# A chain of four transformer parts on one core: another routing tail, one-hot spread and norm, and first products on both halves of the tokens at once

## The chip, the cores and the metric

The kernel runs on one core of one Trainium2 chip. A core has TensorE (PE in the rows; PEld is its loading of weights), VectorE (DVE), ScalarE (ACT), GpSimd (POOL) and SyncE (SP), which work from queues of their own, 16 DMA engines, an SBUF of 128 partitions and the PSUM into which matmuls accumulate. The metric is the device time of one execution in microseconds (us), the median of the runs.

## The reference

256 tokens of width 1024 pass through five parts, each added to its input: a convolution and gated linear attention ("even"), a PEER layer, a gated softmax attention ("odd"), a second PEER layer, and a block with sparse and stick-breaking attention and a feed-forward part (1024 to 4096 to 1024, relu squared). The change touches the two PEER layers, the norms and the feed-forward part:

```python
def peer_ffn(h, wq, keys, u, v):
    q = (h @ wq).reshape(B, S, PEER_HEADS, 2, half)
    s1 = jnp.einsum('bshd,hnd->bshn', q[..., 0, :], keys[:, 0])
    s2 = jnp.einsum('bshd,hnd->bshn', q[..., 1, :], keys[:, 1])
    v1, i1 = lax.top_k(s1, 16)
    v2, i2 = lax.top_k(s2, 16)
    cand = (v1[..., :, None] + v2[..., None, :]).reshape(B, S, 8, 256)
    sc, j = lax.top_k(cand, 16)
    e1 = jnp.take_along_axis(i1, j // 16, axis=-1)
    e2 = jnp.take_along_axis(i2, j % 16, axis=-1)
    experts, gates = e1 * 128 + e2, jax.nn.softmax(sc, axis=-1)
    ...
    act = jax.nn.gelu(jnp.einsum('td,ted->te', ht, u[et]))
    return jnp.einsum('te,ted->td', gt * act, v[et])

    # feed-forward part of the last block
    ff = jnp.square(jax.nn.relu(u2 @ mlp_w1)) @ mlp_w2
```

## The kernel before

**Products.** All large products are taken with f32 split in a high and a low part (`split`, L98 on ScalarE for the high part, L101 for the low part on VectorE or GpSimd), in three matmuls: high by high, high by low, low by high. `hH` and `hL` are the parts of the normed tokens, transposed: 128 rows of the width by 256 tokens for each of KD = 8 pieces. `wload` fetches 512 KB of weights for two products and splits them (`hu`/`lu` and `hv`/`lv` by the ring of buffers in turn); `K.rings` says which engine takes a ring's low parts.

**A PEER layer** (`peer`) computes all 16384 experts densely, as 128 row blocks of 128 hidden units, and gates them by a matrix G that is zero but for the chosen experts. `first(n)` takes 24 matmuls of 256 columns (L768) into `pA` and a Gelu into `A` (L771); `gated(n)` multiplies by G and splits the product into CH and CL (L776, L98, L101); `second(n)` adds the product with v in 12 matmuls of 512 columns (L790, L791, L794) into `po`. 40 first products (RUN) of each half of 64 row blocks are taken ahead, during the routing and the spread; the other 24 stand in the loop over n, so 48 per layer and 96 in the kernel. In the loop a step is one `gated`, one `first` and one `second`, and in the second layer every other step has a piece of the next block's modulation (`ada.one`, L1062).

**Routing** (`routing`) searches the 16 best of the scores by rounds of MAX, MATCH_REPLACE and MAX_INDEX on VectorE. Behind the last search stands the tail: the places j become row and column numbers (L712 to L718), each as a mask against 16 ranks (L734) times the indices (L737), summed by 16 matmuls (L739) per 128 tokens and kind; the softmax gates (L722 to L727) are turned by TensorE (L731). `ahead(5)` puts five first products in front of these on TensorE, `ahead(3)` three more in between.

**Spread** (`spread`): in 32 steps of 8 tokens VectorE builds one-hots of the row number (L811), of the column number (L813) and the first times the gates' high and low parts (L816, twice); 16 small matmuls (L825) make G of them. Three of four steps take one of the first products.

**Norms** (`norm_rows`): per 128 tokens scale, transpose, split to hH and hL; between them the weights of the next products are split. The last block's feed-forward part takes its first products in `gemm_T`, 24 matmuls of 256 columns (L163), then relu and square.

The order on each engine is that of the program, but for the places where `issue_after` and `keep_in_program_order` set it. The lines that set the order in the tail:

```python
    for t in range(2):
        ahead(5 - 2 * t)
        tp = K.ps.tile([128, 3, 128], F, name="pB")
        nc.tensor.transpose(tp[:, 2], e[:, t], K.ident)
        for k in range(2):
            ...
```

Of the kernel before, what the change touches and what calls it, by code (L numbers as in the profile page):

```python
# [30 lines left out]
KD = 8  # L31
S = 256
# [12 lines left out]
class Kit:  # L45


    def __init__(self, ctx, tc, I):
# [23 lines left out]
        self.hH = self.cst.tile([128, KD, S], R, name="hH")  # L72
        self.hL = self.cst.tile([128, KD, S], R, name="hL")
# [21 lines left out]
    def split(self, H, L, src, eng=None):  # L95
# [5 lines left out]
        return (eng or nc.vector).tensor_sub(L, src, H.bitcast(F))  # L101
# [16 lines left out]
    def wsplit(self, raw, ring, n, parts=(0, 1), eng=None):  # L118
# [3 lines left out]
        for i in parts:  # L122
            m = min(1024, n - 1024 * i)
            if m > 0:
                H.append(pool.tile([128, 1024], R, name="h" + ring))
                L.append(pool.tile([128, 1024], R, name="l" + ring))
                with self.tc.issue_after(self.hold.pop().ins) if self.hold and not self.pinning else nullcontext():
                    self.split(H[-1][:, :m], L[-1][:, :m], raw[i][:, :m], eng or own)
# [16 lines left out]
    def gemm_T(self, w, groups, xH, xL, evac, kd=KD, ring=None, psum=None, tags=("pA",), share=1):  # L145
# [5 lines left out]
        for g0 in range(groups[0], groups[1], per):  # L151
            n = min(per, groups[1] - g0)
            H, L = self.wload(w[:, g0:g0 + n].rearrange("p a b -> p (a b)"), ring, n * kd * 128)
            for i in range(n):
# [10 lines left out]
                evac(g0 + i, out)  # L165

# [68 lines left out]
    def norm_rows(self, g, shift=None, early=(), after=None, sooner=False):  # L235
# [8 lines left out]
        W, outs = [], []  # L244
        if sooner:
            self.pinning = True
            W = [self.wsplit(*w, eng=nc.vector) for w in raw]
# [3 lines left out]
        for tb in range(2):  # L251
# [9 lines left out]
            elif after is not None:  # L261
# [3 lines left out]
                else:  # L265
                    self.next = [self.wsplit(*nxt, eng=nc.gpsimd)]
# [13 lines left out]
            if not tb and not sooner:  # L280
# [342 lines left out]
def routing(K, l, grid, rt, new_psum, e1T, e2T, gP, ahead):  # L623
# [10 lines left out]
    nc.gpsimd.tensor_copy(grid, K.iota[:, :, None].to_broadcast([128, 128, 2]))  # L634
# [58 lines left out]
    for h in range(1, 8):  # L693
# [15 lines left out]
    jj = rt.tile([128, 2, 2, 128], U32)  # L709
    jb = rt.tile([128, 2, 2, 128], B)  # L710
    Jf = J.rearrange("p t h r -> p t (h r)")
    nc.vector.tensor_scalar(jj[:, 0], Jf, 4, None, op0=OP.logical_shift_right)  # L712
    nc.vector.tensor_scalar(jj[:, 1], Jf, 2, None, op0=OP.logical_shift_right)
    nc.vector.scalar_tensor_tensor(jb[:, 0], jj[:, 1], -9.0, jj[:, 0], op0=OP.add, op1=OP.max)
    nc.vector.tensor_scalar(jj[:, 0], Jf, 3, None, op0=OP.bitwise_and)
    nc.vector.tensor_scalar(jj[:, 1], Jf, 12, None, op0=OP.bitwise_and)
    nc.vector.scalar_tensor_tensor(jj[:, 1], Jf, 48.0, jj[:, 1], op0=OP.is_lt, op1=OP.mult)
    nc.vector.tensor_add(jb[:, 1], jj[:, 0], jj[:, 1])  # L718
    e = rt.tile([128, 2, 128])
    sm = rt.tile([128, 2, 8])  # L720
    g = e.rearrange("p t (a b) -> p t a b", b=16)
    nc.vector.tensor_sub(g, SC, SC[:, :, :, 0:1].to_broadcast([128, 2, 8, 16]))  # L722
    nc.scalar.activation(g, g, AF.Exp)
    nc.vector.tensor_reduce(sm, g, axis=AX.X, op=OP.add)
    nc.vector.reciprocal(sm, sm)
    nc.vector.tensor_scalar(sm, sm, GATE, None, op0=OP.mult)
    nc.vector.tensor_mul(g, g, sm[:, :, :, None].to_broadcast([128, 2, 8, 16]))  # L727
    for t in range(2):
        ahead(5 - 2 * t)
        tp = K.ps.tile([128, 3, 128], F, name="pB")  # L730
        nc.tensor.transpose(tp[:, 2], e[:, t], K.ident)  # L731
        for k in range(2):
            eq = eqs[t][k]
            nc.vector.tensor_tensor(eq, jb[:, k, t].rearrange("p (h r) -> p h r", r=16)[:, None]  # L734
# [5 lines left out]
        ts = slice(t * 128, t * 128 + 128)  # L740
        nc.scalar.activation(e1T[:, ts], tp[:, 0], AF.Copy)
        nc.scalar.activation(e2T[:, ts], tp[:, 1], AF.Copy)
        nc.scalar.activation(gP[:, 0, ts], tp[:, 2], AF.Copy)
        nc.vector.tensor_sub(gP[:, 1, ts], tp[:, 2], gP[:, 0, ts])


def peer(K, l, ada=None):
    tc, nc, I = K.tc, K.nc, K.I
    hH, hL = K.hH, K.hL
    with tc.tile_pool(name="pe", bufs=1) as pe, tc.tile_pool(name="pw", bufs=2) as pw:  # L750
        G = pe.tile([128, HALF, S], F, name="G")
        e1T, e2T = (pe.tile([128, S], B, name=n) for n in ("e1T", "e2T"))
# [857 lines left out]
```

## Time and profile before

| what | us |
|---|---|
| median of 3 runs (lowest, highest) | 2345.95 (2345.46, 2348.6) |
| the profiled execution | 2346.62 |
| its span | 2344.8 |
| TensorE busy in the span | 2293.3 (98%) |
| VectorE busy | 1595.6 (68%) |
| ScalarE busy | 1262.6 (54%) |
| GpSimd busy | 714.3 (30%) |
| weight loads of TensorE | 2080.4 (89%) |

The mean granted clock of TensorE is 0.992 of full speed. The profile is of one execution; the span runs from its first to its last instruction. A busy TensorE is not a TensorE at its best: the time between the starts of two matmuls tells what one costs, since their recorded durations overlap. In the rows below "x24" is the count of equal instructions in a row, the time behind it is that of all of them, and a bracket tells how long the engine stood idle before and who ended that.

### The profile page before, as it was taken

What the parts mean: (1) busy time and instruction counts of PE and PEld (TensorE: products, weight loads), DVE (VectorE), ACT (ScalarE), POOL (GpSimd) and SP (SyncE); (2) the same over time, 40 slices, a digit from 0 to 9 for tenths busy, and PEclk for the clock granted to TensorE, in tenths of its full rate; (3) what the DMA queues carried; (4) which work ended last, traced back from release to release, by engine and by line L of the source; (5) the groups of instructions that cost most, each with busy time, mean ns of one, the idle gap of its engine ahead of it and who ended that gap; (6) DMA issues with size and microseconds to landing.
All of it is one profiled execution on the core that took longest, in us unless ns stands there. A gap on an engine that the chain in (4) does not pass through costs nothing.

```text
span 2344.8 us, 43309 instructions
## 1 busy us (share of the span) xinstructions
PE 2293.3 (98%) x17000; PEld 2080.4 (89%) x17000; DVE 1595.6 (68%) x3124; ACT 1262.6 (54%) x2046; POOL 714.3 (30%) x327
## 2 busy tenths in 40 slices
PE   9999899999999999999989999999999999998999
PEld 8879799988999988887979998899999888887997
DVE  6949898566875556644789955679555663667754
ACT  6654455555555555675455555555555554565542
POOL 4236203444001444552840244410044442300000
PEclk9999999999999999999989999999999999999999
DMA  6235346655456665642634676554666565334652
GB/s 244 90 131 176 127 145 243 237 200 193 163 169 234 236 214 195 212 135 66 205 127 150 207 244 211 195 177 152 223 234 223 198 206 184 131 108 152 220 195 91
DMA packets 119387, 424.63 MB, mean 181 GB/s; under 512 B 14155, under 2 KB 17037, under 8 KB 118798
## 3 DMA queue, kind: packets, MB, share of 16 engines
q1 hardware_dynamic: 119180, 421.86, 53.4%
q8 instruction: 133, 2.18, 0.4%
q14 instruction: 72, 0.59, 0.1%
q10 hardware_dynamic: 2, 0.00, 0.0%
HBM read 420.72 MB, written 2.66 MB: 181 GB/s over the span
## 4 chain that ended last, share of the span: by engine, by line
PE 45%; DVE 5%; ACT 1%; issue 0%; DMA 0%; POOL 0%; SPq 0%; ACTq 0%; POOLq 0%; DVEq 0%
PE pA L768 14%; PE pA L163 5%; PE po L791 5%; PE po L794 5%; PE po L790 5%; PE pB L163 2%; PE pB L825 1%; PE pA L204 1%; PE pA L205 1%; PE pA L203 1%; PE pB L205 1%; PE pB L204 1%; PE pB L203 1%; DVE G L653 1%; DVE G L650 1%; DVE G L651 1%
## 5 line engine op out<-in xcount | busy, mean ns | idle before, releaser
L101 POOL TENSOR_TENSOR lu<-raw,hu 128x1024 fp32r<-128x1024 f32 x229 | 569.0, 2488 | 1164.9 <-ACT hu L98 1046.3
L98 ACT ACTIVATE hu<-raw 128x1024 fp32r<-128x1024 f32 x348 | 368.3, 1060 | 347.6 <-PE pA L768 248.7
L98 ACT ACTIVATE hv<-raw 128x1024 fp32r<-128x1024 f32 x340 | 360.0, 1060 | 198.7 <-PE pA L768 87.3
L101 DVE TENSOR_TENSOR lv<-raw,hv 128x1024 fp32r<-128x1024 f32 x310 | 386.3, 1248 | 91.7 <-ACT hv L98 88.5
L768 PE MATMUL pA<-hH,hu 128*128 128x256 f32 x1408 | 398.7, 283 | 2.1 <-ACT A L771 1.7
L768 PE MATMUL pA<-hH,lu 128*128 128x256 f32 x1408 | 394.2, 280 | 0.9 <-DVE lu L101 0.6
L768 PE MATMUL pA<-hL,hu 128*128 128x256 f32 x1408 | 393.6, 280 | 0.0
L101 DVE TENSOR_TENSOR CL<-AG,CH 128x256 fp32r<-128x256 f32 x256 | 205.9, 805 | 258.0 <-PE po L794 132.0
L768 PEld LDWEIGHTS pA<-hH,hu 128*128 128x128 f32 x1408 | 264.6, 188 | 6.3 <-ACT A L771 2.1
L768 PEld LDWEIGHTS pA<-hH,lu 128*128 128x128 f32 x1408 | 267.7, 190 | 2.2 <-DVE lu L101 1.5
L768 PEld LDWEIGHTS pA<-hL,hu 128*128 128x128 f32 x1408 | 265.3, 188 | 3.4
L790 PE MATMUL po<-hv,CH 128*128 128x512 f32 x688 | 267.7, 390 | 0.0
L791 PE MATMUL po<-lv,CH 128*128 128x512 f32 x688 | 267.5, 389 | 0.0
L98 ACT ACTIVATE CH<-AG 128x256 fp32r<-128x256 f32 x256 | 106.8, 418 | 271.2 <-PE po L791 268.4
L794 PE MATMUL po<-hv,CL 128*128 128x512 f32 x688 | 211.9, 389 | 0.0
L101 DVE TENSOR_TENSOR lu<-raw,hu 128x1024 fp32r<-128x1024 f32 x119 | 145.5, 1223 | 62.5 <-ACT hu L98 61.6
L768 PE MATMUL pA<-hH,hv 128*128 128x256 f32 x640 | 183.0, 286 | 0.0
L768 PE MATMUL pA<-hH,lv 128*128 128x256 f32 x640 | 178.7, 279 | 0.0
L768 PE MATMUL pA<-hL,hv 128*128 128x256 f32 x640 | 178.5, 279 | 0.0
L794 PEld LDWEIGHTS po<-hv,CL 128*128 128x128 f32 x688 | 129.2, 188 | 26.8
L791 PEld LDWEIGHTS po<-lv,CH 128*128 128x128 f32 x688 | 129.1, 188 | 23.2
L790 PEld LDWEIGHTS po<-hv,CH 128*128 128x128 f32 x688 | 129.0, 188 | 23.1
(641 smaller groups left out, 5224.9 us busy)
## 6 DMA issues: line engine op xcount, KB each, us to landing
raw<-in_p_u_dram SPq DMA_DIRECT2D x256, 512.0 KB, 3.6
raw<-in_p_v_dram SPq DMA_DIRECT2D x256, 512.0 KB, 4.4
raw<-in_b_m_dram SPq DMA_DIRECT2D x64, 512.0 KB, 3.6
raw<-in_b_ada_dram SPq DMA_DIRECT2D x48, 512.0 KB, 3.4
raw<-in_b_wT_dram SPq DMA_DIRECT2D x33, 512.0 KB, 3.3
raw<-in_p_wq_dram SPq DMA_DIRECT2D x32, 512.0 KB, 3.9
raw<-in_od_wT_dram SPq DMA_DIRECT2D x17, 512.0 KB, 3.5
raw<-in_ev_wT_dram SPq DMA_DIRECT2D x13, 512.0 KB, 6.0
```

Of the source, the lines that this page charges most:

```text
L98: i = nc.scalar.activation(H, src, AF.Copy)
L101: return (eng or nc.vector).tensor_sub(L, src, H.bitcast(F))
L163: nc.tensor.matmul(out, a, b[:, k], start=c == 0, stop=c == 3 * kd - 1)
L203: nc.tensor.matmul(po[tb][c], x, h, start=i == 0 and k == 0, stop=False)
L204: nc.tensor.matmul(po[tb][c], x, l, start=False, stop=False)
L205: nc.tensor.matmul(po[tb][c], y, h, start=False, stop=last and k == 3)
L650: nc.vector.max_index(io[:, 0:8], vo[:, 0:8], src)
L651: nc.vector.match_replace(w, vo[:, 0:8], src, LOWEST)
L768: nc.tensor.matmul(ps, a[:, ks], b[:, k], start=c == 0, stop=c == 23)
L790: nc.tensor.matmul(po[tb][dh], CH[:, ts], H[:, ds], start=n == 0, stop=False)
L791: nc.tensor.matmul(po[tb][dh], CH[:, ts], L[:, ds], start=False, stop=False)
L794: nc.tensor.matmul(po[tb][dh], CL[:, ts], H[:, ds], start=False, stop=n == 127)
```

## The change

Five things are changed. (1) The tail of the routing takes the tokens' halves and the two kinds one after the other: numbers, mask and product for k = 0, then for k = 1, with the gates behind the masks of the first half and their transpose last; from the tail on, VectorE takes the low parts of both rings; the wider candidates are spread over the last two heads. (2) In the spread the three compares become one operation over a table `eT` of the row number and the column number, this one stored two times,, and the two products with the gates one. (3) `both` is new: a product in 16 matmuls, 8 of a high weight with hH and hL side by side (512 columns, into two halves of a PSUM tile) and 8 of a low weight with hH (256 columns); ScalarE copies one half and VectorE adds the other. The 96 first products of the loops and 28 of the feed-forward part's 32 row blocks go this way; the first products ahead stay as they were, and C has three buffers instead of four. (4) hH and hL are two halves of one tile. (5) In the norms the low parts of the next weights go from GpSimd to VectorE, behind hL, and where `sooner` is set only the first part of the weights is split early.

The diff, cut to its core:

```diff
-        self.hH = self.cst.tile([128, KD, S], R, name="hH")
-        self.hL = self.cst.tile([128, KD, S], R, name="hL")
+        self.hh = self.cst.tile([128, 2, KD, S], R, name="hh")
+        self.hH, self.hL = self.hh[:, 0], self.hh[:, 1]
...
+    def both(self, out, parts, tag):
+
+
+        nc = self.nc
+        p = self.ps.tile([128, 2, S], F, name=tag)
+        for k in range(KD):
+            h, l = parts(k)
+            if k:
+                nc.tensor.matmul(p[:, 0], l, self.hH[:, k], start=False, stop=False)
+            nc.tensor.matmul(p, h, self.hh[:, :, k], start=k == 0, stop=k == KD - 1)
+            if not k:
+                nc.tensor.matmul(p[:, 0], l, self.hH[:, k], start=False, stop=False)
+        nc.scalar.activation(out, p[:, 1], AF.Copy)
+        nc.vector.tensor_add(out, out, p[:, 0])
...
-            W = [self.wsplit(*w, eng=nc.vector) for w in raw]
+            W = [self.wsplit(*w, (0,), nc.vector) for w in raw]
...
-                    self.next = [self.wsplit(*nxt, eng=nc.gpsimd)]
+                    self.next = [self.wsplit(*nxt, eng=nc.vector, later=lows)]
...
+            for low in lows:
+                low()
+            if not tb:
...
-        if h == 7:
+        if h > 5:
             with K.tc.issue_after(last[0].ins):
-                wider(0, 6)
+                wider(4 * h - 24, 2 * h - 8)
...
     for t in range(2):
         ahead(5 - 2 * t)
+        K.rings = {r: (K.ring, nc.vector) for r in "uv"}
+
+        jj = rt.turn("jj", [128, 2, 128], U32)
+        jb = rt.turn("jb", [128, 2, 128], B)
+        Jf = J[:, t].rearrange("p h r -> p (h r)")
         tp = K.ps.tile([128, 3, 128], F, name="pB")
-        nc.tensor.transpose(tp[:, 2], e[:, t], K.ident)
         for k in range(2):
+            if k:
+                nc.vector.tensor_scalar(jj[:, 0], Jf, 3, None, op0=OP.bitwise_and)
+                nc.vector.tensor_scalar(jj[:, 1], Jf, 12, None, op0=OP.bitwise_and)
+                nc.vector.scalar_tensor_tensor(jj[:, 1], Jf, 48.0, jj[:, 1], op0=OP.is_lt, op1=OP.mult)
+                nc.vector.tensor_add(jb[:, 1], jj[:, 0], jj[:, 1])
+            else:
+                nc.vector.tensor_scalar(jj[:, 0], Jf, 4, None, op0=OP.logical_shift_right)
+                nc.vector.tensor_scalar(jj[:, 1], Jf, 2, None, op0=OP.logical_shift_right)
+                nc.vector.scalar_tensor_tensor(jb[:, 0], jj[:, 1], -9.0, jj[:, 0], op0=OP.add, op1=OP.max)
             eq = eqs[t][k]
-            nc.vector.tensor_tensor(eq, jb[:, k, t].rearrange("p (h r) -> p h r", r=16)[:, None]
+            nc.vector.tensor_tensor(eq, jb[:, k].rearrange("p (h r) -> p h r", r=16)[:, None]
                                     .to_broadcast([128, 16, 8, 16]),
                                     ranks[:, :, None].to_broadcast([128, 16, 8, 16]), op=OP.is_equal)
             nc.vector.tensor_mul(eq, eq, xe[:, t, :, k].rearrange("p h c r -> p c h r"))
             for c in range(16):
                 nc.tensor.matmul(tp[:, k], eq[:, c].rearrange("p h r -> p (h r)"), identB, start=c == 0, stop=c == 15)
-        ts = slice(t * 128, t * 128 + 128)
-        nc.scalar.activation(e1T[:, ts], tp[:, 0], AF.Copy)
-        nc.scalar.activation(e2T[:, ts], tp[:, 1], AF.Copy)
-        nc.scalar.activation(gP[:, 0, ts], tp[:, 2], AF.Copy)
-        nc.vector.tensor_sub(gP[:, 1, ts], tp[:, 2], gP[:, 0, ts])
+        if not t:
+            g = e.rearrange("p t (a b) -> p t a b", b=16)
+            nc.vector.tensor_sub(g, SC, SC[:, :, :, 0:1].to_broadcast([128, 2, 8, 16]))
+            nc.scalar.activation(g, g, AF.Exp)
+            nc.vector.tensor_reduce(sm, g, axis=AX.X, op=OP.add)
+            nc.vector.reciprocal(sm, sm)
+            nc.vector.tensor_scalar(sm, sm, GATE, None, op0=OP.mult)
+            nc.vector.tensor_mul(g, g, sm[:, :, :, None].to_broadcast([128, 2, 8, 16]))
+        nc.tensor.transpose(tp[:, 2], e[:, t], K.ident)
+        ts = slice(t * 64, t * 64 + 64)
+        row, col, gate = (tp[:, j].rearrange("p (t i) -> p t i", i=2) for j in range(3))
+        nc.scalar.activation(eT[:, ts, 0], row, AF.Copy)
+        nc.scalar.activation(eT[:, ts, 1:3], col[:, :, None].to_broadcast([128, 64, 2, 2]), AF.Copy)
+        nc.scalar.activation(gP[:, ts, 0], gate, AF.Copy)
+        nc.vector.tensor_sub(gP[:, ts, 1], gate, gP[:, ts, 0])
...
+        eT = pe.tile([128, S // 2, 3, 2], B, name="eT")
+        gP = pe.tile([128, S // 2, 2, 2], P, name="gP")
...
+            if wide:
+                src = A[n]
+                K.both(src, lambda k: (H[:, k * 128:k * 128 + 128], L[:, k * 128:k * 128 + 128]), "pA")
...
-                    o1 = pw.tile([128, TOK // 2, HALF, 2], P, name="o1", bufs=1)
-                    o2 = pw.tile([128, TOK // 2, 128, 2], P, name="o2")
+                    pairs = lambda x: x[:, t0 // 2:(t0 + TOK) // 2, :, None]
+                    o = pw.tile([128, TOK // 2, 3, HALF, 2], P, name="o")
                     og = pw.tile([128, TOK // 2, 2, HALF, 2], P, name="og")
-                    nc.vector.tensor_tensor(o1, grid[:, None, h0:h0 + HALF].to_broadcast([128, TOK // 2, HALF, 2]),
-                                            pairs(e1T)[:, :, None].to_broadcast([128, TOK // 2, HALF, 2]), op=OP.is_equal)
-                    nc.vector.tensor_tensor(o2, grid[:, None].to_broadcast([128, TOK // 2, 128, 2]),
-                                            pairs(e2T)[:, :, None].to_broadcast([128, TOK // 2, 128, 2]), op=OP.is_equal)
-                    for c in range(2):
-                        nc.vector.tensor_mul(og[:, :, c], o1,
-                                             pairs(gP[:, c])[:, :, None].to_broadcast([128, TOK // 2, HALF, 2]))
-                    late.append((ts, o2, og))
+                    full = [128, TOK // 2, 3, HALF, 2]
+                    nc.vector.tensor_tensor(o, grid.rearrange("p (j n) i -> p j n i", n=HALF)[:, None].to_broadcast(full),
+                                            pairs(eT).to_broadcast(full), op=OP.is_equal)
+                    full = [128, TOK // 2, 2, HALF, 2]
+                    nc.vector.tensor_mul(og, o[:, :, 0, None].to_broadcast(full), pairs(gP).to_broadcast(full))
+                    late.append((ts, o[:, :, 1:3].rearrange("p t j n i -> p t (j n) i"), og))
...
-                    first(n + RUN)
+                    first(n + RUN, wide=True)
...
+            if ps is None:
+                H, L = cur
+                K.both(r, lambda k: [z[g % 2][:, k * 128:k * 128 + 128] for z in (H, L)], "pB" if g % 2 else "pA")
+                ps = r
...
-        K.gemm_T(I["b2_m1"], (2, 30), K.hH, K.hL, act, tags=("pA", "pB"))
+        for g in range(2, 30):
+            if g % 2 == 0:
+                cur = K.wload(flat(I["b2_m1"][:, g:g + 2]))
+            act(g, None)
```

In the order of the second layer's tail, VectorE has before, from the last search on (G stands for the pieces of a work area carved from it):

```order
L653 MAX_INDEX G<-G 128x8
L722 TENSOR_TENSOR G<-G 128x256
L712 TENSOR_SCALAR G<-G 128x256
L713 TENSOR_SCALAR G<-G 128x256
L714 SCALAR_TENSOR_TENSOR G<-G 128x256
L715 TENSOR_SCALAR G<-G 128x256
L716 TENSOR_SCALAR G<-G 128x256
L734 TENSOR_TENSOR G<-G 128x2048
L717 SCALAR_TENSOR_TENSOR G<-G 128x256
L724 TENSOR_REDUCE G<-G 128x16
L718 TENSOR_TENSOR G<-G 128x256
```

and after the change, where L672 is the last MAX_INDEX, L756 the first operation of the gates, L748 the mask and L751 its product:

```order
L744 TENSOR_SCALAR G<-G 128x128
L672 MAX_INDEX G<-G 128x8
L745 TENSOR_SCALAR G<-G 128x128
L756 TENSOR_TENSOR G<-G 128x256
L746 SCALAR_TENSOR_TENSOR G<-G 128x128
L101 TENSOR_TENSOR lv<-raw,hv 128x1024
L748 TENSOR_TENSOR G<-G 128x2048
L739 TENSOR_SCALAR G<-G 128x128
L751 TENSOR_TENSOR G<-G 128x2048
L740 TENSOR_SCALAR G<-G 128x128
L758 TENSOR_REDUCE G<-G 128x16
```

The mask and its product moved ahead of the second kind's numbers and of the gates, the numbers are halves, and a low part of weights (lv) now stands between.

GpSimd from the second layer's routing to the end of its loops, as a difference (lu and lv are low parts of weights; 80 of the 82 in a row are those of the loops):

```order
 L101 TENSOR_TENSOR lu<-raw,hu 128x1024 x2
 L101 TENSOR_TENSOR lv<-raw,hv 128x1024 x3
-L101 TENSOR_TENSOR lu<-raw,hu 128x1024 x2
-L101 TENSOR_TENSOR lv<-raw,hv 128x1024 x2
 L101 TENSOR_TENSOR lu<-raw,hu 128x1024 x82
```

Four subtractions left GpSimd's queue; two of the tail stay.

TensorE in the tail of the second layer after the change: the masks' matmuls of the second kind (L753, each with its load of weights) begin after ten matmuls of a first product (L797) that follow the first kind's sixteen:

```order
L753 LDWEIGHTS G
L753 MATMUL pB<-G 128x128
L797 MATMUL pA<-hh,hv 128x256 x2
L797 MATMUL pA<-hh,lv 128x256
L797 MATMUL pA<-hh,hv 128x256 x2
L797 MATMUL pA<-hh,lv 128x256
L797 MATMUL pA<-hh,hv 128x256 x2
L797 MATMUL pA<-hh,lv 128x256
L797 MATMUL pA<-hh,hv 128x256
L753 LDWEIGHTS G
L753 MATMUL pB<-G 128x128
```

Before, the gates' transpose (L731) stood ahead of all 32 mask matmuls, and nothing between these.

TensorE in a step of the loop before, the end of a product and the start of the second ones:

```order
L768 MATMUL pA<-hH,hu 128x256
L768 MATMUL pA<-hL,hu 128x256
L768 MATMUL pA<-hH,lu 128x256
L768 MATMUL pA<-hH,hu 128x256
L768 MATMUL pA<-hL,hu 128x256
L768 MATMUL pA<-hH,lu 128x256
```

and after, a whole product's beginning (hh is the tile of both halves):

```order
L177 MATMUL pA<-hh,hu 128x512
L179 MATMUL pA<-hh,lu 128x256
L176 MATMUL pA<-hh,lu 128x256
L177 MATMUL pA<-hh,hu 128x512
L176 MATMUL pA<-hh,lu 128x256
L177 MATMUL pA<-hh,hu 128x512
```

Three matmuls of 256 columns became one of 512 and one of 256, eight times per product.

## Rows read from the trace of the kernel before

**Rows 1.** The page: its first line, and busy time of each engine.

```profile
span 2344.8 us, 43309 instructions
...
PE 2293.3 (98%) x17000; PEld 2080.4 (89%) x17000; DVE 1595.6 (68%) x3124; ACT 1262.6 (54%) x2046; POOL 714.3 (30%) x327
```

**Rows 2.** Waits of TensorE: waiting line, releaser, us in total, times, longest.

```profile
PE pB L731 <- DVE G L727: 21.2, 2, 10.6
PE pA L293 <- DVE hL L101: 3.6, 6, 1.1
```

**Rows 3.** Busy time by stretch: us; PE, PEld, DVE, ACT, POOL; clock, DMA share, GB/s.

```profile
1203.00:1216.60 13.60, 5.30 (x41) 5.24 (x42) 13.51 (x17) 0.62 (x3) 3.18 (x2) 0.50 0.29 104
1236.00:1306.00 70.00, 70.00 (x903) 69.23 (x900) 66.09 (x127) 38.40 (x67) 0.00 (x0) 1.00 0.45 152
1320.00:1440.00 120.00, 119.82 (x781) 109.95 (x782) 77.70 (x119) 61.45 (x89) 52.25 (x21) 1.00 0.73 251
...
2177.00:2250.00 73.00, 73.00 (x647) 73.00 (x646) 52.91 (x81) 44.30 (x82) 0.00 (x0) 1.00 0.63 205
```

**Rows 4.** Timeline of TensorE in the second layer's tail: start, us, instruction.

```profile
1197.70 0.38 PE L768 MATMUL pA<-hH,hu 128*128 128x256 f32 x1 [0.84 <-ACT A L771]
...
1211.30 0.47 PE L731 MATMUL pB<-cid,G 128*128 128x128 f32 x1 [10.59 <-DVE G L727]
1211.57 3.62 PE L739 MATMUL pB<-G 128*128 128x128 bf16 x32
...
1224.11 1.95 PE L739 MATMUL pB<-G 128*128 128x128 bf16 x32
```

**Rows 5.** Timeline of VectorE in the same tail.

```profile
1194.23 2.48 DVE L712 TENSOR_SCALAR G<-G 128x256 uint32<-128x256 uint32 x1
...
1207.38 0.41 DVE L717 SCALAR_TENSOR_TENSOR G<-G 128x256 uint32<-128x256 uint32 x1
...
1208.54 1.16 DVE L737 TENSOR_TENSOR G<-G 128x2048 bf16<-128x2048 bf16 x1
```

**Rows 6.** Timeline of GpSimd: in the tail, in a loop, at the last norm.

```profile
1191.62 4.95 POOL L101 TENSOR_TENSOR lu<-raw,hu 128x1024 fp32r<-128x1024 f32 x2 [6.42 <-ACT hu L98]
...
1201.31 4.87 POOL L101 TENSOR_TENSOR lu<-raw,hu 128x1024 fp32r<-128x1024 f32 x2
...
1379.16 2.41 POOL L101 TENSOR_TENSOR lu<-raw,hu 128x1024 fp32r<-128x1024 f32 x1 [3.15 <-ACT hu L98]
...
2163.76 5.44 POOL L101 TENSOR_TENSOR lv<-raw,hv 128x1024 fp32r<-128x1024 f32 x2 [106.09 <-ACT hv L98]
```

**Rows 7.** The chain that ended last, in order of time: start, us, what.

```profile
1215.19 8.97 PE pA L768 x72
...
1325.31 2.83 PE pA L768 x24
1330.85 2.83 PE pA L768 x24
...
1637.76 43.62 PE pA L768 x384
```

**Rows 8.** VectorE in the spread, 1236 to 1306, by shape: count, busy us, mean ns.

```profile
L816 DVE TENSOR_TENSOR og<-o,gP 128x512 f16<-128x512 f16 x54 | 20.4, 421 | 0.0
L813 DVE TENSOR_TENSOR o<-grid,e2T 128x1024 f16<-128x1024 bf16 x27 | 18.6, 688 | 3.4 <-PE pB L825 3.4
L101 DVE TENSOR_TENSOR lu<-raw,hu 128x1024 fp32r<-128x1024 f32 x10 | 12.2, 1222 | 0.0
```

**Rows 9.** Timeline of VectorE in a loop, beside the third entry of GpSimd above.

```profile
1379.98 0.68 DVE L1062 SCALAR_TENSOR_TENSOR raw<-raw,pB 128x512 f32<-128x512 f32 x1
...
1380.88 0.97 DVE L101 TENSOR_TENSOR CL<-AG,CH 128x256 fp32r<-128x256 f32 x1 [0.21 <-PE po L794]
```

**Rows 10.** Timeline of VectorE at the last norm: the two halves' hL.

```profile
2159.87 1.29 DVE L101 TENSOR_TENSOR hL<-raw,hH 128x512 fp32r<-128x512 f32 x2
...
2165.66 4.10 DVE L101 TENSOR_TENSOR hL<-raw,hH 128x512 fp32r<-128x512 f32 x2
```

More of the change, by code (lines that the diff above doesn't have):

```diff
@@ L93, in warm, with split @@
             self.nc.tensor.matmul(p, self.still, self.still, start=True, stop=True)
-    def split(self, H, L, src, eng=None):
+    def split(self, H, L, src, eng=None, later=None):
         nc = self.nc
@@ L100, in split @@
             self.hold = [self.tc.keep_in_program_order(i)] * HELD
-        return (eng or nc.vector).tensor_sub(L, src, H.bitcast(F))
+        low = lambda: (eng or nc.vector).tensor_sub(L, src, H.bitcast(F))
+        return low() if later is None else later.append(low)
     def wraw(self, ap, ring=None, n=2048):
@@ L116, in raw, with wsplit @@
         return pool.tile([128, 1024], F, name="raw", bufs=bufs)
-    def wsplit(self, raw, ring, n, parts=(0, 1), eng=None):
+    def wsplit(self, raw, ring, n, parts=(0, 1), eng=None, later=None):
         pool, own = self.rings[ring]
@@ L127, in wsplit @@
                 with self.tc.issue_after(self.hold.pop().ins) if self.hold and not self.pinning else nullcontext():
-                    self.split(H[-1][:, :m], L[-1][:, :m], raw[i][:, :m], eng or own)
+                    self.split(H[-1][:, :m], L[-1][:, :m], raw[i][:, :m], eng or own, later)
         return H, L
@@ L620, with routing @@
 GATE = 32768.0
-def routing(K, l, grid, rt, new_psum, e1T, e2T, gP, ahead):
+def routing(K, l, grid, rt, new_psum, eT, gP, ahead):
     nc, I = K.nc, K.I
@@ L633, in routing @@
     late()
-    nc.gpsimd.tensor_copy(grid, K.iota[:, :, None].to_broadcast([128, 128, 2]))
+    for o, n in ((0, HALF), (HALF, 128)):
+        nc.gpsimd.tensor_copy(grid[:, o:o + n], K.iota[:, 0:n, None].to_broadcast([128, n, 2]))
     pfx = new_psum()
@@ L762, in first @@
             H, L = (z[n % 2] for z in u[0])
[L763 to L771 removed]
+            A[n] = pw.tile([128, S], F, name="A", bufs=RUN)
+            if wide:
+                src = A[n]
+                K.both(src, lambda k: (H[:, k * 128:k * 128 + 128], L[:, k * 128:k * 128 + 128]), "pA")
+            else:
+                src = K.ps.tile([128, S], F, name="pA")
+                c = 0
+                for k in range(KD):
+                    ks = slice(k * 128, k * 128 + 128)
+                    for a, b in ((H, hH), (H, hL), (L, hH)):
+                        nc.tensor.matmul(src, a[:, ks], b[:, k], start=c == 0, stop=c == 23)
+                        c += 1
+            nc.scalar.activation(A[n], src, AF.Gelu)
         def gated(n):
[L774 removed]
+            C[n] = pw.tile([128, S], R, name="CH", bufs=3), pw.tile([128, S], R, name="CL", bufs=3)
             c = pw.tile([128, S], F, name="AG")
@@ L802, in spread @@
             late = []
+            if h0:
+                nc.vector.tensor_scalar(eT[:, :, 0], eT[:, :, 0], -float(h0), None, op0=OP.add)
             for t0 in range(0, S + TOK, TOK):
@@ L833, in peer @@
             new_psum = lambda: pfx.enter_context(tc.tile_pool(name="pfx", bufs=2, space=PSUM))
[L834 removed]
+            routing(K, l, grid, Carve(G.rearrange("p a b -> p (a b)")), new_psum, eT, gP, ahead)
         ppo = ExitStack()
```

37 lines of the change are left out of this document (3 added, 34 removed).

## The prediction

> **What bounds the kernel now.** I began with the page. TensorE is busy 98% of a span of 2344.8 us, VectorE 68%, ScalarE 54%, GpSimd 30% [rows 1]: what can be gained is time in which TensorE idles, runs at the lower clock, or spends more than it must on an instruction. The profiled execution took 2346.62 us, 1.8 beyond its span and 0.7 above the median of 2345.95; the sum is made on its own time and 0.7 is taken off at the end.
>
> Second, the waits of TensorE. One wait is far above the others: 21.2 us in two pieces, TensorE at the gates' transpose (L731) for VectorE's product L727, once for each peer layer. The next one, for hL of the norms, is 3.6 us in six pieces [rows 2]. All else that stops TensorE is smaller.
>
> Third, the clock by stretch. In 1203 to 1216.6 the granted clock is 0.50, which is the level of 1.2 GHz; in the spread, the loops and the feed-forward part it is 1.00, 2.4 GHz [rows 3]. The low stretch lies behind the long wait, so the wait costs twice.
>
> Fourth, this tail of the routing from near, in the second peer. TensorE waits 0.84 us at 1197.70, then 10.59 us until 1211.30, then its 32 mask matmuls take 3.62 us where the same 32 take 1.95 at 1224.11 [rows 4]. VectorE meanwhile runs integer operations of 256 elements: 2.48 us each at 1194.23, but 0.41 for the same size at 1207.38 [rows 5]. The difference is GpSimd: it subtracts low parts from 1191.62 on, 2.4 to 2.5 us each, six in a row until 1206.2 [rows 6]. So five small operations of VectorE (L712 to L716) were stretched from some 0.4 to 2.4 us, 10 us in all, which is the wait itself.
>
> Fifth, the chain of waits for what a product costs. In the loops the 24 matmuls of a product take 2.83 us and a step 5.54 (1325.31 to 1330.85); in one long stream 384 of them take 43.62, that is 2.73 for 24, at the same clock [rows 7]. The 12 matmuls of 512 columns that fill the rest of a step take 5.54 - 2.83 = 2.71, 226 ns each, while the 256 column ones cost 118 in a loop and 114 in a stream: two of these are 227 to 236.
>
> **Part 1, the tail.** Lost per peer now: 10.59 + 0.84 + (3.62 - 1.95) = 13.1, and (8.97 - 3 x 2.73) = 0.8 in the 72 matmuls behind it that begin at the low clock [rows 4, 7]: 13.9 us. After: four of GpSimd's six subtractions go to VectorE, at 1.22 each [rows 8], so GpSimd is out of the way some 10 us earlier. VectorE's rows from the last search to the first mask product are three half-size integer operations, L756, one low part, compare and multiply: 3 x 0.3 + 0.4 + 1.22 + 2 x 1.16 = 4.8 us [rows 5, 8]. The five products that TensorE has in hand end near 1200.7 (1211.30 - 10.59); the last search ends near 1194, so the first masks are ready near 1199 to 1201.5, the later if the first two subtractions still stretch two operations: TensorE waits 0 to 0.8. The second set is where I expect a wait. Between its masks and the first ones VectorE has five half-size or smaller operations, two of 0.41, one low part, compare and multiply: 5 x 0.2 + 0.8 + 1.2 + 2.3 = 5.3, less 0.07 to 0.1 overlap for each, 4.8; TensorE has the 16 mask matmuls (1.0) and about ten of a product (1.1). A wait of 2.7. For the other 128 tokens TensorE has some three products (8 us) against two low parts, three small operations and a pair of masks (5.3): none, or up to 1.2 us if a product's own low part is late. A low clock after a wait this short would cost another 1.7 at most. In all 2.7 to 6.4 are left; I take 3.5, so 10.4 gained per peer, **-21** for two. Bounds: -10 (half of it comes back as such waits) and -26 (nearly all of it goes).
>
> **Part 2, 96 products of the loops in 16 instead of 24 instructions.** No matmul with different column counts alternating stands in the trace. The columns are the same. Bound below: each 512 at 0.227 and each 256 at 0.118, 8 x 0.345 = 2.756; bound above: 256 at 0.1133, 2.72 [rows 7]. Against 2.83 that is 0.074 to 0.11, so 7.1 to 10.6 us for 96; nearest is a stream, since a load of weights now lies behind 512 columns at every second instruction. I take 2.74: **-8.6**. The lower bound of zero (columns alone count) is a rival. A copy (ScalarE) and an add (VectorE) come in per product: VectorE is busy 77.70 of 120 us there and ScalarE 61.45 [rows 3]; a step adds about 0.42 to each of 5.54, and both keep over a quarter free. Hidden; without cover it would be 0.4 x 96 = 40 us. Three instead of four buffers for C hold back nothing: a C lives about two steps.
>
> **Part 3, the spread.** Four VectorE operations become two with the same elements. By the rows, 1024 cost 0.688 and 512 cost 0.421 [rows 8], 0.267 per 512 more; so 1536 cost 0.955 and the pair 1.64 instead of 1.95. TensorE is busy 70.00 of 70 us there [rows 3]: **0**, as VectorE only gets freer (66.09 busy, 27 steps of 2.45 against 2.59 of TensorE's).
>
> **Part 4, the norms.** Beside GpSimd's pair at the last norm two low parts of hL take 4.10 us instead of 1.29 [rows 6, 10]; TensorE waits for such hL in all 3.6 us in six places [rows 2]. Taking the low parts of the next weights behind hL on VectorE removes up to 2.8 us of lateness at each of two norms. Behind it VectorE is later with the next weights by 2 x 1.22, with work of TensorE in front. I take **-3** (bounds 0 and -5, the waits and what of the low clock goes with them).
>
> **Part 5, 28 products of the feed-forward part.** TensorE is there 73.00 of 73 us, at the stream's price, 28 x (0 to 0.036) = 0 to +1.0; the last product's way out is longer by a copy and an add. **+0.5**. VectorE goes from 52.91 to about 64 of 73, ScalarE from 44.30 to about 55 [rows 3].
>
> Sum: -21 - 8.6 - 3 + 0.5 = -32.1; 2346.6 - 32.1 - 0.7 = 2313.8, rounded **2314**.
>
> **The rivals.**
> - Half the tail. Four more low parts on VectorE (4.9 us) stand in the very queue that TensorE waits for, and if the wait at the second masks is long enough, the low clock stays. Then 5 per peer are gained: -32 + 11 = **2325**. For it: VectorE has no idle time in this stretch [rows 5]. Against: the three small operations per mask are cheap once GpSimd is quiet.
> - Columns alone. The loop's 2.83 may have other reasons than the number of instructions; then part 2 is 0 and the time **2322**. For it: two 256 column matmuls of a stream cost exactly one of 512 [rows 7]. The Trainium skill, TensorE: Matmul & The Clock Gate, section Back-to-back issue gap, gives columns / 2.4 GHz and 2.5 ns for each matmul; eight fewer would save 0.02 us per product, 2.5 us in all, and the time by that is 2320. The rows differ from it: 226 ns at 512 columns where the rule says 216.
> - Slower, by the merged compare. If one operation over 1536 elements with a four-level pattern ran at the f32 rate (1024 in 1.22 us [rows 8]), the pair would cost 1.83 + 1.22 = 3.05, VectorE's step 2.45 - 1.95 + 3.05 = 3.55 against 2.59, so 0.96 x 128 steps = +123: **2437**. It decides once the pair costs over 2.09. For it: no row shows the new pattern. Against: the innermost pairs are as now, and L813 with its broadcasts has the fast rate.
> - Slower, by the evacuation. If the new add is held by GpSimd as the split of C is (0.97 at 1380.88), up to a whole GpSimd operation of 2.41, VectorE's step in the loop is 3.59 + 0.4 + 2.4 = 6.4 against 5.54 [rows 3, 6, 9], +0.85 x 96 = 82: **2404**. It decides once the add costs over 1.95. Against: L1062, with one input in PSUM, took 0.68 for 512 elements in the middle of a GpSimd operation [rows 9]. The Trainium skill, SBUF — State Buffer, section on two separate sides, says the same: VectorE with two SBUF inputs and a GpSimd operation that reads SBUF exclude one another; the add reads one input from PSUM, and by that it is free.
>
> **How the numbers follow.** As forecast (2307 to 2321) 0.62; half the tail 0.13; columns alone 0.09; more gained than that, below 2307, 0.05; several gains absent together, within 0.2% (4.7 us, about what a measurement of this kernel can tell from no change) 0.04; the compare 0.04; the evacuation 0.03. Faster 0.89, same 0.04, slower 0.07. The range of 2304 to 2332 takes in the first three and the bounds of the tail and the loops, and leaves out the slower ones and the largest gain.
>
> **What would show it.** Right: the wait at the gates' transpose gone from TensorE's waits, one of 2 to 4 us at the second masks in its place, and no stretch at 0.50 behind it; a loop step of 5.43 to 5.47; the compare at 0.95 and og at 0.69; hL never at 2 us apiece; TensorE full in the feed-forward part. Wrong: a loop step of 5.54, waits at the masks of over 5 us per peer, TensorE waiting for og or for A.

## The result and the profile after

The changed kernel is slower: median 2367.88 us (2367.16 to 2371.38, 4 runs) against 2345.7 (4 runs) before, ratio 1.0088 (1.0075 to 1.0101), 22 us where 32 less were forecast. The tail did what was predicted; ScalarE lost more than that further on.

The page of the changed kernel, first line and busy time, beside [rows 1]:

```profile
span 2365.5 us, 41434 instructions
...
PE 2309.8 (98%) x16008; PEld 2045.5 (86%) x16008; DVE 1619.3 (68%) x3025; ACT 1332.1 (56%) x2203; POOL 670.8 (28%) x312
```

ScalarE is busy 70 us longer. The 124 new copies of 0.38 can be 48 of these at most; the rest is unexpected. Waits of TensorE in the changed kernel, beside [rows 2]:

```profile
PE pS L1349 <- ACT QZ L1210: 6.7, 3, 2.9
PE pB L1200 <- ACT sgm L1135: 3.8, 1, 3.8
...
PE pB L753 <- DVE G L751: 3.4, 4, 1.3
```

The 21.2 us at the gates' transpose are gone and 3.4 at the masks stand in their place. The first two rows stood at 0.2 and 1.7 before: TensorE waits for ScalarE in the last block, in code that the diff does not touch. There the groups of ScalarE's table loads tell why (ACT_TABLE_LOAD, which the trace has under the line of the function that follows it):

```profile
L332 ACT ACT_TABLE_LOAD x6 | 7.7, 1283 | 0.1
L323 ACT ACT_TABLE_LOAD x5 | 6.4, 1283 | 1.4 <-PEq L1635 1.3
L799 ACT ACT_TABLE_LOAD x5 | 6.4, 1283 | 0.1
L935 ACT ACT_TABLE_LOAD x4 | 5.1, 1283 | 0.1
L936 ACT ACT_TABLE_LOAD x4 | 5.1, 1283 | 0.1
...
```

In all 42 loads of 1.283 us where the kernel before has 17. The 25 more, one for a Gelu and 24 for Ln and Exp, cost 32.1 us of ScalarE. They begin at one place, the end of the second layer's loops. ScalarE's timeline there, changed kernel:

```profile
1794.00 0.39 ACT L180 ACTIVATE A<-pA 128x256 f32<-128x256 f32 x1 [1.70 <-PE pA L177]
...
1794.56 1.28 ACT L323 ACT_TABLE_LOAD   x1
1795.85 1.28 ACT L799 ACT_TABLE_LOAD   x1
1797.14 0.42 ACT L799 ACTIVATE A<-A 128x256 f32<-128x256 f32 x1
```

and the same place before:

```profile
1809.91 0.37 ACT L771 ACTIVATE A<-pA 128x256 f32<-128x256 f32 x1
...
1810.44 1.28 ACT L305 ACT_TABLE_LOAD   x1
1811.74 0.42 ACT L98 ACTIVATE CH<-AG 128x256 fp32r<-128x256 f32 x1
```

`K.table()` (the load at L305, now L323) fetches one table that serves both Ln and Exp, once, behind the last Gelu (L771, now L799). The wide product's Gelu has to wait for VectorE's add, so in the second layer the preload came to stand in front of it; the Gelu fetched its own table at 1795.85, and from then on each change between Ln and Exp in the norms and the attention fetched one (L935 and L936 four times each, by turns). In the first layer the Gelu kept its place.

Lining up equal matmuls of the two traces gives where the time went: +0.3 us ahead of the first tail; -10.1 and -10.6 in the two tails, to the first small matmul of the spread; 0 in the spreads; +0.6 and +0.4 in the two layers' loops; +4.3 at the norm behind the first layer; +33.2 from the end of the second layer's loops to the feed-forward part; +2.6 in this. In all +20.7, the difference of the spans.

The loop, TensorE's timeline of the changed kernel, one step from its first wide matmul to that of the next:

```profile
1752.07 0.39 PE L177 MATMUL pA<-hh,hu 128*128 128x512 f32 x1
...
1752.77 0.28 PE L176 MATMUL pA<-hh,lu 128*128 128x256 f32 x1
1752.88 0.40 PE L177 MATMUL pA<-hh,hu 128*128 128x512 f32 x1
1753.12 0.28 PE L176 MATMUL pA<-hh,lu 128*128 128x256 f32 x1
...
1757.63 0.39 PE L177 MATMUL pA<-hh,hu 128*128 128x512 f32 x1
```

A step takes 5.56 us against 5.54 in [rows 7]. From 1752.77 to 1753.12 a pair takes 0.35: the 256 columns still cost 0.118, and the 512 now cost 0.235 instead of 0.227 (medians of the loop). Stretches of loop and feed-forward part, beside [rows 3]:

```profile
1310.00:1415.00 105.00, 105.00 (x530) 88.92 (x530) 70.87 (x122) 58.12 (x96) 47.65 (x20) 1.00 0.75 254
2190.00:2270.00 80.00, 80.00 (x474) 70.33 (x472) 64.30 (x110) 54.55 (x111) 0.00 (x0) 1.00 0.61 194
```

TensorE is full in both and no engine came near its limit: the evacuation is hidden, the matmuls themselves got no cheaper.

### The profile page after: what moved, and what is told of

Its sections match the earlier page's. It is cut to its first block, busy times and chain, and to the rows that moved or that the text cites. A ratio compares the mean times of both kernels' runs of the same rounds, so it can differ in the third digit from the quotient of the medians.

```text
span 2365.5 us, 41434 instructions
## 1 busy us (share of the span) xinstructions
PE 2309.8 (98%) x16008; PEld 2045.5 (86%) x16008; DVE 1619.3 (68%) x3025; ACT 1332.1 (56%) x2203; POOL 670.8 (28%) x312
## 4 chain that ended last, share of the span: by engine, by line
PE 46%; ACT 3%; DVE 2%; issue 1%; POOL 0%; POOLq 0%; DVEq 0%; ACTq 0%
PE pA L797 9%; PE po L819 5%; PE po L818 5%; PE po L822 5%; PE pA L177 5%; PE pA L164 4%; PE pA L176 2%; PE pB L852 1%; PE pB L177 1%; PE pA L219 1%; PE pA L221 1%; PE pA L220 1%; PE pB L164 1%; PE pB L221 1%; PE pB L219 1%
## 5 line engine op out<-in xcount | busy, mean ns | idle before, releaser
L101 POOL TENSOR_TENSOR lu<-raw,hu 128x1024 fp32r<-128x1024 f32 x218 | 541.2, 2485 | 1159.0 <-ACT hu L98 1038.1
L101 DVE TENSOR_TENSOR CL<-AG,CH 128x256 fp32r<-128x256 f32 x256 | 219.2, 856 | 227.7 <-ACT CH L98 147.5
L177 PE MATMUL pA<-hh,hu 128*128 128x512 f32 x808 | 292.7, 396 | 0.0
L797 PE MATMUL pA<-hh,hv 128*128 128x256 f32 x1280 | 229.7, 281 | 0.0
L797 PE MATMUL pA<-hh,hu 128*128 128x256 f32 x1280 | 228.9, 281 | 0.0
L176 PE MATMUL pA<-hh,lu 128*128 128x256 f32 x707 | 198.5, 281 | 0.0
L101 DVE TENSOR_TENSOR lu<-raw,hu 128x1024 fp32r<-128x1024 f32 x130 | 158.3, 1221 | 56.0 <-ACT hu L98 55.3
L797 PEld LDWEIGHTS pA<-hh,hv 128*128 128x128 f32 x1280 | 194.8, 189 | 0.2
L797 PEld LDWEIGHTS pA<-hh,hu 128*128 128x128 f32 x1280 | 194.3, 188 | 0.1
L177 PEld LDWEIGHTS pA<-hh,hu 128*128 128x128 f32 x808 | 151.6, 188 | 30.7
L797 PE MATMUL pA<-hh,lv 128*128 128x256 f32 x640 | 178.1, 278 | 0.0
L797 PE MATMUL pA<-hh,lu 128*128 128x256 f32 x640 | 177.9, 278 | 0.0
```

The costliest lines, as they stand in the source:

```text
L101: low = lambda: (eng or nc.vector).tensor_sub(L, src, H.bitcast(F))
L176: nc.tensor.matmul(p[:, 0], l, self.hH[:, k], start=False, stop=False)
L177: nc.tensor.matmul(p, h, self.hh[:, :, k], start=k == 0, stop=k == KD - 1)
L797: nc.tensor.matmul(src, a[:, ks], b[:, k], start=c == 0, stop=c == 23)
```

## The experiments

Each run is compared with runs of the kernel before on the same chip; its median there was 2347.7 to 2348.4 us.

**The preload two steps later** (changed kernel):

```diff
-                    if n + RUN == 127:
-                        K.table()
+                if n + RUN == 129:
+                    K.table()
```

> The changed kernel with the preload of ScalarE's table two steps of the loop later, behind the last Gelu; all else as changed. Theory 1 (the preload came to stand in front of the last Gelu of the second layer, so the table with Ln and Exp was lost and every Ln and Exp of the last block loads one): 17 table loads instead of 40, 23 x 1.28 = 29 us of ScalarE less, most of it on the path: about 2343 us (2339 to 2348), level with the kernel before. Theory 2 (the wide products with their copy and add, and ScalarE's greater load, cost the time): no change, 2368.

Measured 2338.63 us, ratio 0.9958 (0.9946 to 0.9971). One line moved takes 29 us off the changed kernel and makes it 0.3 to 0.5% faster than the kernel before, slightly more than theory 1 gave. 17 loads are left.

**The reverse on the kernel before:** in the second layer the preload stands ahead of `first(127)`.

```diff
+                    if l and n + RUN == 127:
+                        K.table()
                     first(n + RUN)
...
-                    if n + RUN == 127:
+                    if not l and n + RUN == 127:
                         K.table()
```

> The kernel before with one edit: in the second layer the preload of ScalarE's table stands before the last first product's Gelu instead of behind it. Theory 1: some 42 table loads as in the changed kernel, about 2370 us (2364 to 2375). Theory 2: 2346 to 2348, one reload of 1.28 us.

Measured 2374.42, ratio 1.011 (1.0095 to 1.0125), 26 us more. The order of two ScalarE instructions is shown as the cause from both sides; theory 2 falls.

**Narrow products in the loops** (changed kernel, `first(n + RUN)` without `wide`):

> The changed kernel with the loops' 96 products in 24 matmuls again (the feed-forward part stays wide); with it the last Gelu is ahead of the preload again. Theory 1: as the run with the late preload, less 0 to 2 us, since a loop step took 5.558 us wide and 5.545 narrow: 2341 (2337 to 2346). Theory 2: the evacuations gone from the loops bring 2325, the old forecast without its loop term.

Measured 2337.11, ratio 0.9955 (0.9942 to 0.9968), not to be told from wide products with a late preload, and 17 loads again with the preload in its old line: without the wide products of the loops the Gelu stays ahead of it. Of the 8.6 us that I gave 8 instructions fewer per product, 96 times, nothing shows.

**The norms' edit alone** on the kernel before:

> The kernel before with the norms' edit alone (low parts of the next weights on VectorE behind hL, and only the first part of the weights early where sooner is set). My old step: 3 us less, 2343. Theory 3 (VectorE's low parts delay the scaled tokens that TensorE waits for; the changed trace lost 4.4 us at the norm behind the first layer and some 3.4 beside table loads at that behind the second): 7 to 9 us more, 2353.

Measured 2350.58, ratio 1.0013 (1.0004 to 1.0022): a loss of 1 to 5 us, neither my gain nor theory 3's size. VectorE at the last norm in this run, beside [rows 10]:

```profile
2165.28 1.22 DVE L101 TENSOR_TENSOR lv<-raw,hv 128x1024 fp32r<-128x1024 f32 x1
2166.42 1.28 DVE L278 TENSOR_TENSOR raw<-pB,mod 128x512 f32<-128x512 f32 x2
2167.62 1.21 DVE L101 TENSOR_TENSOR lv<-raw,hv 128x1024 fp32r<-128x1024 f32 x1
2168.75 1.28 DVE L101 TENSOR_TENSOR hL<-raw,hH 128x512 fp32r<-128x512 f32 x2
```

hL takes 1.28 instead of 4.10, as I had it, but two low parts of weights now stand ahead of it on VectorE. From the scaling of these tokens (2162.77 before, 2163.95 here) to the end of hL it takes 6.1 us instead of 7.0: of the 2.8 that GpSimd's quiet gave, 0.9 are left. The first of the two low parts also stands ahead of L278, which makes what hH is split from, and for that TensorE now waits longer. In this run:

```profile
PE pA L294 <- ACT hH L98: 3.8, 4, 1.7
```

and before, where hL made it wait 3.6 us [rows 2] instead of 3.3 here:

```profile
PE pA L291 <- ACT hH L98: 2.9, 5, 1.0
```

In each of the last two norms the wait for the second half's hH is 1.68 us in this run's trace and 0.72 before.

**Three buffers of C alone** on the kernel before (`bufs=3` for CH and CL):

> The kernel before with three buffers for C instead of four, and nothing else. My old step: 0, since a C lives two steps. Theory 4 (the end of a layer keeps four C, 124 to 127, for both halves of the tokens; with three, the split of 127 waits until 124 is done with the second half, so the first half's sum is complete some 2 us later and the norm behind it loses its cover): 3 to 4 us at each of the two layers' ends, 6 to 8 in all, 2353.

Measured 2352.9, ratio 1.0016 (1.0008 to 1.0025), 2 to 6 us. ScalarE at the end of the first layer, this run:

```profile
965.73 0.42 ACT L98 ACTIVATE CH<-AG 128x256 fp32r<-128x256 f32 x1 [3.93 <-PE po L791]
```

and in the kernel before:

```profile
959.37 0.42 ACT L98 ACTIVATE CH<-AG 128x256 fp32r<-128x256 f32 x1 [1.21 <-PE po L791]
```

The last split waits 3.93 us for a buffer instead of 1.21. By the traces this run loses 2.3 us at each layer's end, less than theory 4's 3 to 4.

**Tail and spread alone** (changed kernel; narrow products everywhere, norms as before, and the last three instead of four products by halves, which three buffers allow):

```diff
-                if LAG <= n < 126:
+                if LAG <= n < 127:
                     second(n - LAG)
         for tb in range(2):
-            for n in range(124, 128):
+            for n in range(125, 128):
                 second(n, (tb,))
```

> The changed kernel with the routing tail and the spread alone: all products in 24 matmuls, norms as before, and the last three instead of four products taken by halves so that three buffers of C suffice. If tail and spread are what gains and theories 1 and 4 hold the rest: 2346 - 21 = 2325, and 0 to 3 more for a cover of three products (4.1 us) instead of four (5.4): 2325 to 2329. If the losses at the layers' ends come from something else, 2333 as the late preload with narrow products.

Measured 2331.92, ratio 0.9933 (0.992 to 0.9946), 16 us under the kernel before, which took 2348.4 here: between the two expectations, and nearer the second. By the traces each layer's end still costs 1.9 and 1.5 us against the kernel before, so three products by halves save little of the 2.3 that three buffers cost.

**The same with the norms' edit:**

> The run with tail and spread alone, plus the norms' edit. By the run of the norms' edit alone (ratio 1.0013): 1 to 5 us above it, about 2330. My old step: 3 below it.

Measured 2335.69, ratio 0.9946 (0.9934 to 0.9958): 4 us worse by the medians, though the intervals overlap. Not all of it is the norms'. The feed-forward part, the same code with narrow products in both, 50 us of each run, first of tail and spread alone:

```profile
2175.00:2225.00 50.00, 50.00 (x444) 50.00 (x443) 35.54 (x55) 29.79 (x55) 0.00 (x0) 1.00 0.66 198
```

then of the run with the norms' edit:

```profile
2175.00:2225.00 50.00, 50.00 (x427) 50.00 (x426) 35.20 (x54) 29.10 (x54) 0.00 (x0) 1.00 0.64 185
```

444 recorded matmuls of 256 columns against 427, both full and at clock 1.00: 113 ns and 117 ns each. The run with the early preload, whose feed-forward code is that of the kernel before, shows 427 too:

```profile
2230.00:2280.00 50.00, 50.00 (x427) 50.00 (x426) 34.76 (x55) 29.47 (x54) 0.00 (x0) 1.00 0.61 181
```

So the slower spacing comes without any change to that part; over 28 products it is worth 3 us, which is about how far single executions of one kernel differ.

**One and two small matmuls ahead of each product of the loops** (kernel before, `K.warm(1)`, `K.warm(2)`):

> The kernel before with one small matmul (128 columns, bf16, into a spare tile) ahead of each of the 96 products of the loops. Theory 5 (a run of f32 matmuls takes one of two rates per column, 0.443 or 0.459 ns, at its start and keeps it; behind the spread's small matmuls two of three products take the faster one, behind 512 columns of the second products all take the slower): many of the loops' products at 2.72 to 2.75 instead of 2.83, less 0.06 for the small matmul: 2340 to 2346, and in its trace spacings of 113 ns in the loops. Rival (the loops' 118 ns comes from the other engines' work there): spacings stay at 118 and it is 5 to 10 us slower.

> The kernel before with two small matmuls ahead of each product of the loops. With one the spacing stayed at 118 ns and a product cost 0.17 us more. If the entry sets the rate by chance of its phase, a second one can put the products at 113 ns (0.11 less each, 10 us below the run with one); if not, spacings of 118 and some 6 us above it.

Measured 2363.96, ratio 1.0073 (1.0059 to 1.0086), and one run of 2369.39. Neither run is the test that was meant. In the program a small matmul (L93) stands ahead of each product; in the built kernel the 24 of a loop, or 48, all stand in its last 15 to 17 us. L93 in the first loop of the run with one, the columns being span, busy time and count, clock, share of DMA and GB/s:

```profile
349.00:468.00 119.00, 0.00 (x0) 1.00 0.71 236
468.00:484.00 16.00, 3.77 (x24) 1.00 0.57 188
```

Only three products of a loop, 12 of the 96, have a small matmul right in front. One of them, in the run with two:

```profile
481.13 0.28 PE L93 MATMUL pB<-still 128*128 128x128 bf16 x2
481.23 0.37 PE L768 MATMUL pA<-hH,hu 128*128 128x256 f32 x1
481.43 0.28 PE L768 MATMUL pA<-hL,hu 128*128 128x256 f32 x1
...
483.93 0.28 PE L768 MATMUL pA<-hH,lu 128*128 128x256 f32 x1
484.05 0.39 PE L790 MATMUL po<-hv,CH 128*128 128x512 f32 x1
```

From 481.43 to 483.93 lie 22 spacings of 0.114: the faster rate, as theory 5 has it, and all 12 products of either run come to it. Those behind 512 columns stay at 0.118. But the first spacing is 0.20, and the product takes 2.82, no less than the others' 2.83. So theory 5 holds for these 12 and gains nothing there; for the other 84 it was not tested. The small matmuls cost 0.16 us each where they came to stand, not 0.06.

**Wide products with three products by halves** (late preload, norms as changed):

> The changed kernel (wide products in loops and feed-forward part, norms as changed) with the late preload and the last three instead of four products by halves. Theories 1 and 4: 1 to 4 us below the late preload alone, ratio to before 0.994 to 0.9955 (2332 to 2336 beside a before of 2346). If three buffers of C cost nothing in the changed kernel: 0 to 2 above it, since the cover is shorter.

Measured 2338.87, ratio 0.9964 (0.9951 to 0.9977), not to be told from 0.9958 without it, and above the range of theories 1 and 4. Inconclusive, as products by halves with three buffers cost 1.9 and 1.5 us themselves (the run with tail and spread alone).

**The same, matmuls grouped by width:**

```diff
+        w = [parts(k) for k in range(KD)]
+        nc.tensor.matmul(p, w[0][0], self.hh[:, :, 0], start=True, stop=False)
+        for k in range(KD):
+            nc.tensor.matmul(p[:, 0], w[k][1], self.hH[:, k], start=False, stop=False)
+        for k in range(1, KD):
+            nc.tensor.matmul(p, w[k][0], self.hh[:, :, k], start=False, stop=k == KD - 1)
```

> As the run before it, with the wide products' matmuls in another order: one of 512 columns, all eight of 256, then seven of 512, so that the widths alternate twice instead of fifteen times. If the alternation keeps a wide product at 0.459 ns a column (theory 6): 512 columns at 227 ns and 256 at 113 to 118, a loop step of 5.44 to 5.48 instead of 5.56, 96 x 0.1 and 28 x 0.1 = 10 to 12 us less than the run before. If the rate is set otherwise (by what stands ahead of the product): step 5.55, no difference.

Measured 2334.96, ratio 0.9947 (0.9934 to 0.9959). TensorE's timeline in the loop:

```profile
1702.58 0.39 PE L174 MATMUL pA<-hh,hu 128*128 128x512 f32 x1
1702.81 1.08 PE L176 MATMUL pA<-hh,lu 128*128 128x256 f32 x8
1703.73 1.79 PE L178 MATMUL pA<-hh,hu 128*128 128x512 f32 x7
1705.36 0.39 PE L817 MATMUL po<-hv,CH 128*128 128x512 f32 x1
```

The 256 column ones now start 115 ns apart (0.92 / 8; 114 behind the first), but the seven of 512 columns 233 (1.63 / 7). By the medians of 86 steps the product takes 2.78 instead of 2.82, and the twelve matmuls behind it 2.76 instead of 2.74, so the step is 5.54 against 5.56. Alternation is part of what holds the 256 columns at 118, but not what keeps the 512 from 227: of the 10 to 12 us, 4 came by the medians of the runs, and the intervals overlap.

**The same with the norms as before:**

> The run with the wide products' matmuls grouped by width, with the norms as before the change. If the norms' edit costs what its runs gave (0.13% on the kernel before, 0.13% on tail and spread): ratio 0.9934 (0.992 to 0.995), level with tail and spread alone, so that wide products bring nothing in the best arrangement found. If the norms' edit is neutral beside wide products: 0.9947.

Measured 2330.21, ratio 0.9924 (0.991 to 0.9937), the fastest of all, though its interval overlaps that of tail and spread alone. Against its twin with the new norms it gains 4.8 us by the medians. Of the 5.0 between the two traces 3.6 lie in the first ten us, ahead of the first norm. The twin there:

```profile
5.09 3.78 PE L83 MATMUL pA<-raw 1*128 1x512 f32 x4
```

and this run:

```profile
4.99 1.98 PE L83 MATMUL pA<-raw 1*128 1x512 f32 x4
```

The slow start is not the norms': the run with the early preload, which has the old ones, also took 3.78 in its trace, and tail and spread with the new ones 1.98. So three pairs of runs agree that the norms' edit loses, and not in how much: by the traces, from the end of the first layer's loops to the feed-forward part, it is 1.6 us on the kernel before, 4.5 on tail and spread, 1.4 here.

## Why the prediction was wrong

**The step that failed** is in part 2: "A copy (ScalarE) and an add (VectorE) come in per product ... Hidden". I costed the evacuation as time that two engines have to spare, and that held. I did not cost that it moves the Gelu back in ScalarE's queue, past the preload. In the program the Gelu stands ahead of both L1061 and the preload, so an engine's order is not that of the program throughout, as the section on the kernel before has it. The order of the changed kernel as built shows it without a run:

```order
L180 ACTIVATE A<-pA 128x256
L1061 ACTIVATE raw<-pB 48x128
L323 ACT_TABLE_LOAD
L799 ACT_TABLE_LOAD
L799 ACTIVATE A<-A 128x256
```

None of the rivals had it; the slower ones named VectorE. It is worth 29 us (2367.88 to 2338.63), and 26 the other way round on the kernel before, shown by two runs that mirror each other.

The rest of the 53 us between forecast and trace is 10 in the loops (+1 for -8.6), 11 at the norms and the layers' ends (+8 for -3), and 2 in the feed-forward part; the tails came as forecast.

**Part 1, the tail: right.** 10.1 and 10.6 us gained by the traces, 10.4 forecast, and the wait came where I put it, at the second masks. VectorE in the second layer's tail, changed kernel:

```profile
1193.65 1.22 DVE L751 TENSOR_TENSOR G<-G 128x2048 bf16<-128x2048 bf16 x1
...
1195.85 1.22 DVE L101 TENSOR_TENSOR lv<-raw,hv 128x1024 fp32r<-128x1024 f32 x1
1196.99 1.22 DVE L748 TENSOR_TENSOR G<-G 128x2048 bf16<-128x2048 bf16 x1
...
1198.46 1.22 DVE L751 TENSOR_TENSOR G<-G 128x2048 bf16<-128x2048 bf16 x1
```

From one mask product to the next 4.81 us, as computed (4.8). TensorE waits 1.31 for it, half of my 2.7, since the first masks were ready 1.29 ahead of TensorE (1194.87 to 1196.16):

```profile
1196.16 1.07 PE L753 MATMUL pB<-G 128*128 128x128 bf16 x16
1199.73 1.07 PE L753 MATMUL pB<-G 128*128 128x128 bf16 x16 [1.31 <-DVE G L751]
```

The clock stays at 1.00 there, and the 16 mask matmuls take 1.07 (columns as in [rows 3]):

```profile
1200.00:1212.00 12.00, 12.00 (x121) 11.96 (x119) 12.00 (x20) 4.86 (x10) 0.00 (x0) 1.00 0.37 120
```

That the sum fits so well is partly luck: of the 3.5 us that I left per layer, the waits at the masks are 1.7, and the rest was not traced.

**Part 2, the products: wrong, the rival "columns alone" is what happened.** Wide and narrow products of the loops cost the same. I read 2.83 against 2.73 in [rows 7] as a price per instruction; it is a price per column (0.459 or 0.443 ns), and 512 columns take it too. By the medians of 86 steps, 84 before, a product takes 2.82 instead of 2.83, grouped by width 2.78, and the twelve matmuls of 512 columns behind it 2.74 and 2.76 instead of 2.72: what the product gained, these lost. The Trainium skill, TensorE: Matmul & The Clock Gate, section Back-to-back issue gap, has a fixed 2.5 ns per matmul, by an estimate 0.02 us for eight fewer and 1.9 us for 96 products. The loops' two medians are 1.5 us apart with the wide products slower, and intervals of 3 us either way neither show it nor exclude it.

The rival that the add is held by GpSimd did not come. The loops' 96 adds, shortest, median and longest in ns:

```profile
L181 DVE TENSOR_TENSOR A<-A,pA x96: 405/418/425, 352.5 to 1794.4; 128x256 f32<-128x256 f32 x96
```

The buffers of C were not free: "a C lives about two steps" holds in the loop, not at its end, where four are kept for the second half (2 to 6 us).

**Part 3, the spread: right.** The merged compare takes 0.955 and og 0.685 (0.955 and 0.688 computed), and TensorE stays full:

```profile
L841 DVE TENSOR_TENSOR o<-grid,eT 128x1536 f16<-128x1536 bf16 x23 | 21.5, 955 | 6.0 <-PE pB L852 6.0
L844 DVE TENSOR_TENSOR og<-o,gP 128x1024 f16<-128x1024 f16 x23 | 15.3, 685 | 0.0
...
1230.00:1290.00 60.00, 60.00 (x785) 59.35 (x784) 53.08 (x62) 33.03 (x57) 0.00 (x0) 1.00 0.45 149
```

**Part 4, the norms: wrong in sign.** Removing the lateness of hL was right row by row (4.10 to 1.28); "Behind it VectorE is later with the next weights" was not: two low parts stand ahead of the second half's hL, one of them ahead of hH, and TensorE waits for that.

**Part 5, the feed-forward part: the term was mis-sized**, +2.6 for +0.5. All 28 wide products ran at 0.459 ns a column; a narrow stream runs at either rate (113 ns in the kernel before, 117 in two of the traces above), so part of this is chance.

What sets the rate at the start of a run of matmuls stays open. It is not the number of instructions and not the alternation of widths alone. What stands ahead counts: in the kernel before, all 90 loop products that can be read behind 512 columns run at 118 ns, and 63 of 96 behind the spread's small matmuls at 113.

## What to carry to other kernels

Where an edit lengthens the way out of a product, follow the instruction at its end through its own engine's queue, past anything placed there once by hand (a table, a mode, a preload): the cost is not its microseconds but what it passes. Before a price is read as one per instruction, look for a row in which the wider instruction stands in the same stretch; here both prices were proportional to columns. A buffer count is checked at the end of a loop, where more are held than in the steady state, and a moved operation at each place in the queue that it lands in. An edit of the order is looked up in the order as built before its run is read: both the preload and the small matmuls stood elsewhere than in the program.

## What was not expected of the hardware

TensorE takes an f32 matmul of a full stretch mostly at one of two rates, 113 or 118 ns for 256 columns and 227 or 235 for 512, both at a granted clock of 1.00; grouped by width, 512 columns lie 233 apart. The same stream of the same kernel's code can show either in another execution (444 against 427 recorded matmuls in 50 us). Behind a small bf16 matmul a product's first spacing is 0.20 us and the later ones come to 0.114, behind 512 columns all are 0.118, and both products take 2.82 or 2.83. A table load of ScalarE takes 1.283 us, and with Ln and Exp by turns it came at each change between them although one table for both had been loaded before.
